# Hybrid SSD and chunk-MLP layer: x issued first, small parameters moved behind the first stage's last chunk, the last tile's h shared between two engines

## The chip, the core and the metric

The kernel runs on one core of one Trainium2 chip. A core has five engines, each with a queue of its own: PE (TensorE, the matrix products; its weight loads are listed apart as PEld), DVE (VectorE), ACT (ScalarE), POOL (GpSimd) and SP (SyncE, which here only issues transfers). Transfers between the chip's memory and the core's SBUF are issued on the queues of SP, ACT and POOL and are carried by 16 DMA engines that all of them share. The metric is the time of the program on the device in microseconds; less is better.

## The reference, cut to what matters

One layer (DEPTH is 1) over 256 latent tokens and 256 context tokens, width 2048. Context and latent tokens are normalized, modulated by adaLN with their own shift and scale, and projected; the latent ones then pass a two-sided SSD group and a chunked gating MLP group, and both meet in one output projection.

```
sc, scc = silu(c), silu(c_ctx)
shift, scale, gate = split(sc @ w_ada + b_ada, 3)          # the same for scc: shift_c, scale_c
hc = rmsnorm(ctx, g_pre) * (1 + scale_c) + shift_c
hx = rmsnorm(x, g_pre) * (1 + scale) + shift
zc = hc @ w_in[:, :XBC_W + DT_W]
zx = hx @ w_in                                              # XBC | dt | z_ssd | u | v | z_mlp
dt = softplus(z[dt columns] + dt_bias);  A = -exp(a_log)
xbc = silu(dwconv_rows(z[XBC columns], conv_w, conv_b))
y = ssd in both directions over xbc, dt, A  (latent starts from the context's final state)
y_a = rmsnorm((y + d_skip * xh) * silu(z_ssd), g_ssd)
y_b = rmsnorm(u * (w_s @ rmsnorm(v, g_v) + b_s) * silu(z_mlp), g_mlp)
out = x + gate * rmsnorm(concat(y_a, y_b) @ w_out, g_post)
```

## The kernel before

Every product with a large weight is made in three passes: each factor is split into a high part (a rounded copy, hi) and a low part (the rest, lo), and hi·hi, hi·lo and lo·hi are summed (mm3, lines 141 to 145).

The first stage, on which the change works, does four things at once. It reads x and ctx, transposed, into the tile xT (512 tokens, 16 tiles of 128 channels, four loads of 1 MB). It makes the norm's statistics. It computes shift and scale from w_ada. And it makes the first part of the projection for seven of the 32 column tiles of XBC and for the dt columns, tile of channels by tile of channels: row kt needs xT's tile kt, its shift and scale (hab), and the chunk wst[kt] of w_in (960 columns, 480 KB).

Transfers in that stage. On SP: sc2 (c and c_ctx, 16 KB, line 184), then xT (line 296), then, in the order of their need, chunks of w_ada ("ada", 1 MB each or two halves of 512 KB, lines 81 and 303) and of wst (lines 292 and 308). On ACT: pc (line 107), one tile with all parameters that lie along channels: 304 columns, of which the first 80 are b_ada and g_pre, used in the first stage, and the rest (from C_GSSD on) g_ssd, g_mlp, b_s, conv_w and conv_b, used later. In row 6 of the first stage ACT issues three more: dtc (dt_bias), A (a_log) and dsk (d_skip), lines 503 to 505, each a short vector spread over 128 partitions.

From line 286 on, PE, DVE, ACT and POOL keep the order in which the program writes their instructions (manual_schedule); ahead of that line, and on SP and the issuing of transfers, the builder orders them. The head of the stage (lines 314 to 361) reads so:

- ACT: silu of sc2 into sc (314), a square root of a constant (315), the copy of cb[0] (331), the first square, the copy of cb[1] (342), then the other squares of xT's even tiles (340).
- DVE: two diagonal tiles made from sc (328), then the squares of xT's odd tiles (338).
- PE: three filler products (warm, 322, 324), the two products of the diagonal tiles that spread c over all partitions (330), then per tile of xT the sum of its squares into pss (344), with a filler after each fourth (322, 346).
- Then pss is transposed (350), summed (352), its root and reciprocal taken (355, 356), and spread again (357, 358) into rb; ada_mm(0) and ada_mm(1) and two fillers follow on PE (359 to 361), and row 0 starts (line 452) when scale_x (388) and make_hs (400, 401) have made its h.

The rows (lines 414 to 445, a list of steps for each row) hold the products of row kt and, between them, the preparation of row kt + 1 or kt + 2: split_hi on ACT and split_lo and split_dt on DVE for the weights, make_h (four pieces on ACT, line 394) or make_hs (each of its two tensors half on ACT, half on DVE, lines 400 and 401) for h, make_hl (404) for its low part, ada_mm on PE and ada_part on DVE (265; its product goes to a junk tile cbj, which is yseg(0), a piece of the later output tile y) and ada_fin for shift and scale. From row 4 on two rows share one unit of shift and scale, so that each odd row prepares the next two tiles. In row 13 the weights of tile 15 come first (the whole chunk in one cast) and then its h in four pieces on ACT; in row 14 the low part of the weights (385) comes ahead of the low part of h (404). Row 15 ends the stage: psdt is copied and transposed to tokens, dtc is added (412), and the second stage, from line 507 on, starts with dt_all (A is used in line 650) and streams w_in's other columns, w_out and the gate's weights in 1 MB loads (line 81), in buffers that overlay those of the first stage.

Of the kernel before, what the change touches and what calls it, by code (L numbers as in the profile page):

```python
# [8 lines left out]
F32 = mybir.dt.float32  # L9
# [6 lines left out]
P = 128  # L16
D = 2048
KT = D // P
# [18 lines left out]
C_BADA, C_GPRE, C_GSSD, C_GMLP, C_BS, C_CW, C_CB, NPC = 0, 48, 64, 80, 96, 112, 272, 304  # L37
# [10 lines left out]
def tile_hybrid_ssd_mlp(  # L48
# [19 lines left out]
    nc = tc.nc  # L68
    ORDER = _tile_order()

    def mkpool(**kw):
        return tc.tile_pool(reuse_waits="tile", **kw)
# [29 lines left out]
    stp = st.enter_context(mkpool(name="stp", bufs=1, side="right"))  # L102
# [1 line left out]


    pc = cpool.tile([P, NPC], F32, name="pc")
    nc.scalar.dma_start(pc, pcols)
    dtc = stp.tile([P, 64], F32, name="dtc")

    ident = cpool.tile([P, P], F32, name="ident")  # L110
    make_identity(nc, ident)
    ones = cpool.tile([P, P], F32, name="ones")
# [34 lines left out]
    def bc(ap, axis, n):  # L147
        u = ap.unsqueeze(axis)
        shp = list(u.shape)
        shp[axis] = n  # L150
        return u.to_broadcast(shp)
# [4 lines left out]
    def yseg(j):  # L156
        return y[:, j // 4, (j % 4) * 512 : (j % 4 + 1) * 512]


    zq = (yseg(2), yseg(3), yseg(7)[:, 0:256])  # L160
    zdt = yseg(1)

    slot = (1, 2, 0, 3)
    zt, e = yseg(5)[:, 0:256], yseg(5)[:, 256:512]
# [1 line left out]
    s2 = yseg(4)[:, 0:256]  # L166
    at = y[:, 0, 256:512].rearrange("p (t h) -> p t h", t=4)
    fold = yseg(7)[:, 256:320]
    A = yseg(7)[:, 320:384]
    nc.vector.tensor_reduce(fold, ident.rearrange("p (g m) -> p m g", g=2), axis=mybir.AxisListType.X, op=ALU.add)  # L170
    acp = ctx.enter_context(mkpool(name="acp", bufs=2, space=PSUM))
    sps = ctx.enter_context(mkpool(name="sps", bufs=6, space=PSUM))
# [8 lines left out]
    sc = stp.tile([P, KT, 32], F32, name="sc")  # L181
    nc.vector.memset(sc, 0.0)
    sc2 = stp.tile([P, KT, 2], F32, name="sc2")
    nc.sync.dma_start(sc2, ccols)
    sqr = st3.tile([P, WST], F32, tag="wst", name="sqr")[:, 0:512], stp.tile([P, 512], F32, name="sqf")
    cb, cbj = (yseg(2), yseg(3)), yseg(0)
    part = {}
# [16 lines left out]
    def ada_load(*cs):  # L204
        for ci in cs:
            if ci >= 2 * NSING and ci % 4 == 3:
                ada_load2(ci)
            else:
                ada_raw[ci] = load_raw(wada[ci], f"ada_{ci}")
# [80 lines left out]
    def wst_load(kt):  # L290
        w = st3.tile([P, WST], F32, tag="wst", name=f"wst{kt}")
        nc.sync.dma_start(w, wst[kt])
        wraw[kt] = w
# [41 lines left out]
    for k in range(KT):  # L335
# [7 lines left out]
        g = k % 4  # L343
# [39 lines left out]
    def split_lo(kt, a=64, b=WST):  # L383
        hi, lo = sp0[kt]
        nc.vector.tensor_tensor(lo[:, a - 64 : b - 64], wraw[kt][:, a:b], hi[:, 64 + a : 64 + b].bitcast(F32), op=ALU.subtract)
# [28 lines left out]
    def row_steps(kt):  # L414


        m = [("m", i) for i in range(-1, NST)]
        if kt == KT - 1:
            out_ = [("m", i) for i in LAST]
            out_.insert(3, ("t", 0))  # L420
            for i in range(2):
                out_.insert(out_.index(("m", 4 + i)) + 1, ("z", i))
            return out_
        n = kt + 1
        c_, d_, l_, h_, e_ = [(w, n) for w in ("c", "d", "l", "h", "e")]
        m0 = [("m", -1), ("p", 0), ("p", 1), ("p", 2), ("w", 0), ("q", 0), ("q", 1), ("q", 2)]
        m1 = [("m", i) for i in range(3, NST)]
        u = (n - NSING) // 2 + NSING
        x = [("x", k) for k in XROW[kt]] if kt < len(XROW) else []
        p = 4 * u - 2 * NSING  # L430
        s_ = [("s", (n, i)) for i in range(2)]
        c1, c2, l1, l2 = [(w, n) for w in ("c1", "c2", "l1", "l2")]
        if n < NSING:
            r = [("r", 2 * n), ("r", 2 * n + 1)]
            q, f = (8, m1[1:2]) if n == 1 else (6, [])
            v = [("v", (NSING, i)) for i in range(4)] if n == NSING - 1 else []
            return (m0[:q] + f + r + [c1, ("k", n), d_, l1] + m1[:1] + [("g", n), ("o", n)] + s_ + [c2] + v[:1] + [e_, l2] + v[1:] + x
                    + m0[q:] + m1[1 + len(f):])
        if kt % 2 == 0:
            v = [("v", (u + 1, i)) for i in range(4)] if n + 1 < KT else []  # L440
            return [d_, l_] + v[:1] + [e_] + v[1:] + m0 + m1
        v = [("v", (u, i)) for i in range(4, 8)] + [("b", u)]
        a = [("a", c) for c in range(p + 1, p + 4)]
        t = v + [c1, ("f", u), d_, s_[0], l1, s_[1], e_, c2, l2, ("c", n + 1)] + x + [("h", (n + 1, i)) for i in range(2)]
        return m0 + m1[:1] + a + t + m1[1:]

    STEPS = {"a": ada_mm, "f": ada_fin, "v": lambda ui: ada_part(*ui), "b": ada_bias, "r": ada_rows, "x": scale_x, "e": make_hl, "s": lambda ni: make_hs(*ni), "k": ada_keep, "g": ada_sum, "o": ada_one,
# [7 lines left out]
    def step(kt, what, i):  # L455
        if what in STEPS:
            STEPS[what](i)
        elif what == "z":
            nc.vector.tensor_copy(zq[i], psx[4 + i])
        elif what == "t":  # L460
            dt_tok()
        elif i < 0:
            dt_mm(kt, 0)
            if kt == KT - 1:
                dt_mm(kt, 1)
        elif what == "w":
            dt_mm(kt, 1)
        elif what in "pq":
            whi, wlo = sp0[kt]
            wh = whi[:, (i + 1) * P : (i + 2) * P]  # L470
            if what == "p":
                nc.tensor.matmul(psx[i], lhsT=wh, rhs=hhi[kt], start=kt == 0, stop=False)
                nc.tensor.matmul(psx[i], lhsT=wlo[:, i * P : (i + 1) * P], rhs=hhi[kt], start=False, stop=False)
            else:
                nc.tensor.matmul(psx[i], lhsT=wh, rhs=hlo[kt], start=False, stop=False)
        else:
            whi, wlo = sp0[kt]
            mm3(psx[i], whi[:, (i + 1) * P : (i + 2) * P], wlo[:, i * P : (i + 1) * P], kt,
                kt == 0 and i < 6, kt == KT - 1 and i != 3, ORDER[FIRST[i]] >= 24)
# [13 lines left out]
    for kt in range(KT):  # L493
        cs = (2 * kt + 6, 2 * kt + 7) if kt + 3 < KT else ()
        q = 0 if kt < NSING - 2 or kt % 2 else 2
        ada_load(*cs[:q])
        if kt < KT - 2:
            wst_load(kt + 2)
        ada_load(*cs[q:])
        for what, i in row_steps(kt):  # L500
            step(kt, what, i)
        if kt == 6:
            nc.scalar.dma_start(dtc, dtp[0:1].partition_broadcast(P))
            nc.scalar.dma_start(A, dtp[1:2].partition_broadcast(P))
            nc.scalar.dma_start(dsk, dskip.partition_broadcast(P))

    st.close()
# [141 lines left out]
    def dt_all():  # L649
        nc.scalar.activation(A, A, AF.Exp)  # L650
        nc.vector.scalar_tensor_tensor(e, zt, -1.0, zt, op0=ALU.mult, op1=ALU.min)
        split_hi(0)
        nc.scalar.activation(e, e, AF.Exp)
        split_lo(0)
        split_hi(1)
        nc.vector.tensor_scalar(s1, e, 2.0, None, op0=ALU.add)
        nc.vector.reciprocal(s1, s1)
        split_hi(2)
        nc.vector.tensor_tensor(s1, s1, e, op=ALU.mult)
        nc.vector.tensor_tensor(s2, s1, s1, op=ALU.mult)  # L660
        nc.vector.tensor_scalar(pl, s2, 2.0 / 15.0, None, op0=ALU.mult)
        split_lo(1)
        for m in (13, 11, 9, 7, 5, 3):
            nc.vector.scalar_tensor_tensor(pl, pl, 2.0 / m, s2, op0=ALU.add, op1=ALU.mult)
        nc.vector.scalar_tensor_tensor(pl, pl, 2.0, s1, op0=ALU.add, op1=ALU.mult)
        nc.vector.scalar_tensor_tensor(dtt.rearrange("p t h -> p (t h)"), zt, 0.0, pl, op0=ALU.max, op1=ALU.add)
        nc.vector.scalar_tensor_tensor(at, dtt, -1.0, bc(A, 1, 4), op0=ALU.mult, op1=ALU.mult)
        split_lo(2)
# [462 lines left out]
    for blk in range(16):  # L1131
# [11 lines left out]
        for u in range(8):  # L1143
            whi, wlo = half(base + blk * 8 + u)
            for kk in range(2):
                k = 2 * u + kk
                w = slice(kk * 512, (kk + 1) * 512)
                for tk in range(2):
                    t = slice(256 + tk * P, 256 + (tk + 1) * P)
# [223 lines left out]
```

## Time and profile before

| what | us |
|---|---|
| median of 3 runs | 984.83 |
| lowest and highest of them | 984.71 and 985.9 |
| the profiled execution | 986.03 |
| its span, first to last instruction | 984.3 |
| PE, DVE, ACT, POOL busy in it | 974.9, 658.2, 498.3, 112.6 |
| memory read over the span | 204.20 MB, 210 GB/s |

A line of the profile's order of time gives the start and the duration of an instruction in us, its engine (ACTq and SPq are the issuing of ACT and SP), the line of the kernel, the operation, the tile written and the tiles read, the shape, how many instructions are merged into the line, and in brackets how long the engine stood idle before it and what ended that. A line of the waits gives who waited for whom, the sum in us, how often, and the longest. A line of the stretches gives the stretch and its length, then busy time and count for PE, PEld, DVE, ACT and POOL, the granted TensorE clock, the busy share of the DMA engines and GB/s. A line of the transfers gives the tile and its source, the queue, how many, the size of each and the median us from issue to landing.

### The profile page before, as it was taken

The numbers are of one execution on the slowest core, as the hardware profiler recorded it, in microseconds if no ns is written. First come the engines' busy times: TensorE is split into PE (matmuls) and PEld (weight loads), VectorE is DVE, ScalarE is ACT, GpSimd is POOL, SyncE is SP. The second block draws the span as 40 slices with busy tenths as digits, with TensorE's granted clock in tenths as the row PEclk, the third lists the DMA queues.
The fourth block names the chain that finished last, engine by engine and source line by source line (L and its number), as shares of the span: only waits on it lengthen the run. The fifth ranks groups of instructions, "written<-read, shape, count | busy, mean of one in ns | idle before, by whom it ended". The sixth has DMA issues, their size and how long they took to land.

```text
span 984.3 us, 13659 instructions
## 1 busy us (share of the span) xinstructions
PE 974.9 (99%) x5306; PEld 786.8 (80%) x5306; DVE 658.2 (67%) x1055; ACT 498.3 (51%) x759; POOL 112.6 (11%) x162
## 2 busy tenths in 40 slices
PE   9999999999999999999999999999999999999997
PEld 4688888787887878787888888887888888888885
DVE  6888798778876675656666766677555564445636
ACT  4344458666575454644445334555565553345522
POOL 0000002541462222133000000000000000000000
PEclk9999999999999999999999999999999999999999
DMA  9999943332333323146877767864455545556722
GB/s 371 416 414 414 403 165 133 114 131 86 129 112 136 138 86 129 61 154 241 305 298 280 269 243 288 298 258 171 173 195 187 176 169 211 189 195 236 276 87 86
DMA packets 32849, 207.26 MB, mean 211 GB/s; under 512 B 4224, under 2 KB 4480, under 8 KB 10128
## 3 DMA queue, kind: packets, MB, share of 16 engines
q1 hardware_dynamic: 29664, 192.71, 52.4%
q0 software_dynamic: 2112, 12.65, 3.6%
q10 hardware_dynamic: 1008, 1.02, 0.3%
q8 instruction: 42, 0.69, 0.3%
q14 instruction: 23, 0.19, 0.1%
HBM read 204.20 MB, written 2.16 MB: 210 GB/s over the span
## 4 chain that ended last, share of the span: by engine, by line
PE 72%; DMA 10%; issue 9%; DVE 5%; ACT 2%; POOL 1%; SPq 0%; DVEq 0%; ACTq 0%; POOLq 0%
PE psx L143 8%; PE psx L145 8%; PE psx L144 8%; PE pa L1150 8%; PE pa L1151 8%; PE pa L1152 8%; DMA wst<-in_wst_dram 5%; PE pm L1197 3%; PE pm L1199 3%; PE pm L1198 3%; PE pq L1199 2%; PE pq L1197 2%; PE pq L1198 2%; PE psc L820 1%; DMA gvb<-in_gv_dram 1%
## 5 line engine op out<-in xcount | busy, mean ns | idle before, releaser
L88 DVE TENSOR_TENSOR lo_w<-w,hi_w 128x1024 fp32r<-128x1024 f32 x173 | 210.3, 1223 | 139.9 <-ACT hi_w L87 139.9
L87 ACT CAST hi_w<-w 128x1024 fp32r<-128x1024 f32 x173 | 182.1, 1052 | 202.6 <-PE pa L1152 131.8
L1150 PE MATMUL pa<-hi_w,hhi 128*128 128x512 f32 x512 | 202.3, 395 | 0.0
L1151 PE MATMUL pa<-lo_w,hhi 128*128 128x512 f32 x512 | 199.4, 390 | 0.5 <-DVE lo_w L88 0.5
L1152 PE MATMUL pa<-hi_w,hlo 128*128 128x512 f32 x512 | 199.5, 390 | 0.0
L143 PE MATMUL psx<-hhi,hi_w 128*128 128x512 f32 (+1 forms) x400 | 153.4, 383 | 0.0
L145 PE MATMUL psx<-hhi,lo_w 128*128 128x512 f32 (+1 forms) x400 | 145.9, 365 | 0.0
L144 PE MATMUL psx<-hlo,hi_w 128*128 128x512 f32 (+1 forms) x400 | 145.7, 364 | 0.0
L1150 PEld LDWEIGHTS pa<-hi_w,hhi 128*128 128x128 f32 x512 | 96.1, 188 | 20.6 <-issue 1.6
L1151 PEld LDWEIGHTS pa<-lo_w,hhi 128*128 128x128 f32 x512 | 96.2, 188 | 20.2 <-DVE lo_w L88 0.9
L1152 PEld LDWEIGHTS pa<-hi_w,hlo 128*128 128x128 f32 x512 | 96.1, 188 | 20.3
L618 DVE SCALAR_TENSOR_TENSOR xbc<-psx,pc,xbc 128x248 f32<-128x248 f32 (+1 forms) x204 | 83.6, 471 | 34.9 <-ACT xbc L602 33.9
L543 DVE TENSOR_TENSOR lo_w<-w,hi_w 128x1024 fp32r<-128x1024 f32 x61 | 77.1, 1270 | 23.6 <-ACT hi_w L537 23.6
L143 PEld LDWEIGHTS psx<-hhi,hi_w 128*128 128x128 f32 x400 | 75.5, 189 | 13.4 <-issue 2.9
L145 PEld LDWEIGHTS psx<-hhi,lo_w 128*128 128x128 f32 x400 | 75.4, 189 | 12.5
L144 PEld LDWEIGHTS psx<-hlo,hi_w 128*128 128x128 f32 x400 | 75.7, 189 | 12.2 <-issue 1.7
L537 ACT CAST hi_w<-w 128x1024 fp32r<-128x1024 f32 x61 | 63.5, 1044 | 25.7 <-PE pa L1152 12.9
L1008 DVE SCALAR_TENSOR_TENSOR junk<-gate,cb 128x2048 bf16<-128x2048 f32 x16 | 36.6, 2290 | 29.2 <-DMA gate<-in_wada_dram 29.2
L1197 PE MATMUL pm<-hi_w,hhi 128*128 128x512 f32 x128 | 49.9, 390 | 0.0
L1198 PE MATMUL pm<-lo_w,hhi 128*128 128x512 f32 x128 | 49.9, 390 | 0.0
L1199 PE MATMUL pm<-hi_w,hlo 128*128 128x512 f32 x128 | 49.7, 389 | 0.0
L377 ACT CAST hi_st<-wst 128x448 fp32r<-128x448 f32 (+2 forms) x26 | 17.2, 679 | 56.9 <-DMA wst<-in_wst_dram 56.9
(269 smaller groups left out, 1392.2 us busy)
## 6 DMA issues: line engine op xcount, KB each, us to landing
w<-in_wlat_dram SPq DMA_DIRECT2D x64, 1024.0 KB, 4.8
w<-in_wout_dram SPq DMA_DIRECT2D x32, 1024.0 KB, 4.8
w<-in_wxbc_dram SPq DMA_DIRECT2D x25, 1024.0 KB, 4.8
ada<-in_wada_dram SPq DMA_DIRECT2D x24, 1024.0 KB, 13.3
gate<-in_wada_dram SPq DMA_DIRECT2D x16, 1024.0 KB, 5.8
ada<-in_wada_dram SPq DMA_DIRECT2D x16, 512.0 KB, 12.0
R<-acs POOLq DMA_DIRECT2D x8, 1024.0 KB, 5.0
wst<-in_wst_dram SPq DMA_DIRECT2D x15, 480.0 KB, 12.1
```

Source lines behind the costliest of these rows:

```text
L87: nc.scalar.copy(hi, raw)
L88: nc.vector.tensor_tensor(lo, raw, hi.bitcast(F32), op=ALU.subtract)
L143: nc.tensor.matmul(ps, lhsT=whi, rhs=hhi[k][:, s], start=start, stop=False)
L144: nc.tensor.matmul(ps, lhsT=whi, rhs=hlo[k][:, s], start=False, stop=False)
L145: nc.tensor.matmul(ps, lhsT=wlo, rhs=hhi[k][:, s], start=False, stop=stop)
L618: nc.vector.scalar_tensor_tensor(ao, zi, cw[:, k : k + 1], ao, op0=ALU.mult, op1=ALU.add)
L1150: nc.tensor.matmul(pa[tk], lhsT=hhi[k][:, t], rhs=whi[:, w], start=k == 0, stop=False)
L1151: nc.tensor.matmul(pa[tk], lhsT=hhi[k][:, t], rhs=wlo[:, w], start=False, stop=False)
L1152: nc.tensor.matmul(pa[tk], lhsT=hlo[k][:, t], rhs=whi[:, w], start=False, stop=k == KT - 1)
L1197: nc.tensor.matmul(p, lhsT=yh[:, t], rhs=whi[:, w], start=j == 0, stop=False)
L1198: nc.tensor.matmul(p, lhsT=yh[:, t], rhs=wlo[:, w], start=False, stop=False)
L1199: nc.tensor.matmul(p, lhsT=yl[:, t], rhs=whi[:, w], start=False, stop=hf == 0 and j == 15)
```

## The change

- x ahead: sc2 leaves SP's queue for ACT's, so that xT's loads are the first on SP. On ACT, sc2 stands behind pc.
- pc in two parts: the first 80 columns at the start, the other 224 in row 14 on ACT.
- dtc and A lose their places (a tile of its own, and a piece of yseg(7)) for two pieces of yseg(0), and are loaded after row 13's steps on SP, behind the last wst chunk, instead of in row 6 on ACT. dsk is loaded in row 14 on ACT, behind the rest of pc.
- In row 13, tile 15's h is made by make_hs (half on DVE) and ahead of the cast of its weights; in row 14, its low part is made first.

```
     pc = cpool.tile([P, NPC], F32, name="pc")
-    nc.scalar.dma_start(pc, pcols)
-    dtc = stp.tile([P, 64], F32, name="dtc")
-
+    nc.scalar.dma_start(pc[:, 0:C_GSSD], pcols[:, 0:C_GSSD])
...
+    dtc, A = yseg(0)[:, 0:64], yseg(0)[:, 64:128]
...
-    A = yseg(7)[:, 320:384]
...
-    nc.sync.dma_start(sc2, ccols)
+    nc.scalar.dma_start(sc2, ccols)
...
         if kt % 2 == 0:
             v = [("v", (u + 1, i)) for i in range(4)] if n + 1 < KT else []
-            return [d_, l_] + v[:1] + [e_] + v[1:] + m0 + m1
+            return ([d_, l_] + v[:1] + [e_] + v[1:] if v else [e_, d_, l_]) + m0 + m1
...
-        t = v + [c1, ("f", u), d_, s_[0], l1, s_[1], e_, c2, l2, ("c", n + 1)] + x + [("h", (n + 1, i)) for i in range(2)]
+        g = [("c", n + 1)] + x + [("h", (n + 1, i)) for i in range(2)]
+        if n == KT - 2:
+            g = [("s", (n + 1, i)) for i in range(2)] + g[:1]
+        t = v + [c1, ("f", u), d_, s_[0], l1, s_[1], e_, c2, l2] + g
...
-        if kt == 6:
-            nc.scalar.dma_start(dtc, dtp[0:1].partition_broadcast(P))
-            nc.scalar.dma_start(A, dtp[1:2].partition_broadcast(P))
+        if kt == KT - 3:
+            nc.sync.dma_start(dtc, dtp[0:1].partition_broadcast(P))
+            nc.sync.dma_start(A, dtp[1:2].partition_broadcast(P))
+        if kt == KT - 2:
+            nc.scalar.dma_start(pc[:, C_GSSD:], pcols[:, C_GSSD:])
             nc.scalar.dma_start(dsk, dskip.partition_broadcast(P))
```

## The prediction

> **What bounds the kernel now.** I read the page first, then the stretches, then the order of time at both ends of the first stage.
>
> ```profile
> span 984.3 us, 13659 instructions
> PE 974.9 (99%) x5306; PEld 786.8 (80%) x5306; DVE 658.2 (67%) x1055; ACT 498.3 (51%) x759; POOL 112.6 (11%) x162
> ...
> q10 hardware_dynamic: 1008, 1.02, 0.3%
> ```
>
> TensorE is busy for 99% of the span, so a gain or loss at the start reaches the end unless a later wait swallows it. The span is 984.3 us, this execution 986.03 (1.7 lie around the span), the median 984.83. I make the sum as a difference and set it on the median.
>
> The view by stretches, cut where the norm statistics end (16.84), where the first product starts (21.85) and where the first stage ends (126.10):
>
> ```profile
> 8.00:16.80 8.80, 8.45 (x41) 2.03 (x40) 4.06 (x6) 5.37 (x10) 0.00 (x0) 1.00 1.00 415
> ...
> 21.85:126.10 104.25, 103.47 (x1061) 82.95 (x1061) 88.19 (x215) 44.41 (x81) 0.00 (x0) 1.00 1.00 405
> 126.10:984.30 858.20, 851.03 (x4064) 696.08 (x4062) 557.88 (x814) 443.95 (x662) 110.23 (x147) 1.00 0.51 183
> ```
>
> From 21.85 to 126.10 the DMA share is 1.00 and PE is busy 103.47 of 104.25 us: transfers and products are both full, tied to within little. So how much PE waits for transfers in there decides what a shift of either is worth. The waits of the weight loads, 15 to 130 us:
>
> ```profile
> PEld psdt L452 <- ACT hhi L400: 1.4, 4, 0.8
> ...
> PEld psada L256 <- DMA ada<-in_wada_dram: 1.0, 2, 0.5
> PEld psada L227 <- DMA ada<-in_wada_dram: 1.0, 2, 0.6
> ...
> PEld psdt L452 <- DVE hlo L404: 0.4, 1, 0.4
> ```
>
> The 0.8 of the first row is row 0's own start; without it they are 3.0 us. A weight load runs ahead of its product, so less is lost: at the last one 0.4 of idle load became about 0.25 of idle PE (the two psdt products quoted below start 0.48 apart; the mean of the long stretch above is 851.03 / 4064 = 0.21). At that ratio some 1.8 us of this stage are waits that would go if transfers led by more. Bounds: 0.5 and 3.0.
>
> **The head, which the change rearranges.** The order of time before the first product:
>
> ```profile
> 0.81 0.38 SPq L184 DMA_DIRECT2D sc<-in_ccols_dram  x1
> ...
> 1.25 2.24 SPq L296 DMA_DIRECT2D xT<-in_xch_dram  x4
> ...
> 2.80 1.28 ACT L314 ACT_TABLE_LOAD   x1 [2.80 <-DMA sc<-in_ccols_dram]
> ...
> 4.36 0.69 DVE L328 TENSOR_TENSOR y<-ident,sc 128x512 f32<-128x512 f32 x1 [0.51 <-ACT sc L314]
> ...
> 6.40 2.33 PE L330 MATMUL pscb<-y,ones 128*128 128x512 f32 x4
> 6.41 0.34 PEld L330 LDWEIGHTS pscb<-y,ones 128*128 128x128 f32 x1 [0.52 <-issue]
> ...
> 7.26 0.21 PEld L330 LDWEIGHTS pscb<-y,ones 128*128 128x128 f32 x1 [0.52 <-DVE y L338]
> 7.71 0.19 PEld L330 LDWEIGHTS pscb<-y,ones 128*128 128x128 f32 x1 [0.24 <-issue]
> 7.91 0.59 ACT L331 COPY y<-pscb 128x512 f32<-128x512 f32 x1 [2.07 <-PE pscb L330]
> ...
> 8.92 0.58 ACT L342 COPY y<-pscb 128x512 f32<-128x512 f32 x1
> ...
> 9.39 1.16 ACT L340 ACTIVATE y<-xT 128x512 f32<-128x512 f32 x2
> ...
> 11.07 0.70 PE L322 MATMUL psw<-ones 128*128 128x256 f32 x2
> ...
> 15.56 0.62 PE L344 MATMUL pss<-y,ones 128*32 128x512 f32 x1
> ...
> 16.56 1.13 PE L322 MATMUL psw<-ones 128*128 128x512 f32 x2
> 16.84 0.72 DVE L350 STREAM_TRANSPOSE y<-pss 128x512 f32<-128x512 f32 x1 [1.68 <-PE pss L344]
> ```
>
> All of ACT, VectorE and TensorE stand in hand-written order behind sc: ACT's table load waits for it, the two diagonal tiles of L328 stand ahead of VectorE's squares, the L330 products ahead of the squares' sums, both copies ahead of ACT's squares. Today sc lands so early that the diagonal tile, ready at 5.05, waits until 6.40 behind the filler products of L322.
>
> **Part 1: x first, sc2 behind pc on ACT's queue.** x is issued at 0.81 instead of 1.25: the transfer stream comes 0.44 us sooner. ACT gets one issue more, while it waits anyway. pc shrinks from 304 to 80 columns, 152 to 40 KB: 0.28 us of stream at 415 GB/s. That is the gain. The cost: the two small loads now travel while x fills all 16 engines. What that does is shown by the three small loads that ACT issues in row 6, under a full stream:
>
> ```profile
> ada<-in_wada_dram SPq DMA_DIRECT2D x16, 512.0 KB, 12.0
> ...
> dtc<-in_dtp_dram ACTq DMA_DIRECT2D x1, 32.0 KB, 5.7
> y<-in_dtp_dram ACTq DMA_DIRECT2D x1, 32.0 KB, 6.8
> sc<-in_ccols_dram SPq DMA_DIRECT2D x1, 16.0 KB, 1.9
> dsk<-in_dskip_dram ACTq DMA_DIRECT2D x1, 16.0 KB, 7.6
> ```
>
> (size, and us from issue to landing), and the issues in order of time:
>
> ```profile
> 68.27 0.34 ACTq L503 DMA_DIRECT2D dtc<-in_dtp_dram  x1
> ...
> 68.65 0.45 ACTq L504 DMA_DIRECT2D y<-in_dtp_dram  x1
> 69.13 0.45 ACTq L505 DMA_DIRECT2D dsk<-in_dskip_dram  x1
> ```
>
> They land at 73.97, 75.45 and 76.73: 1.48 and 1.28 us apart, for 32 and 16 KB, so it isn't bytes. ACT's queue made 1008 packets for seven transfers (these three, pc, three stores): 144 each, nine for each of 16 engines. The big stream then had 4 KB rows; at 415 GB/s over 16 engines one takes 0.158 us, and nine take 1.42. So a small load gets one packet in for each packet of the stream. x has 8 KB rows, 0.316 us each: nine turns are 2.84 us, and pc and sc2, one behind the other, need 5.7. The Trainium skill, "DMA: Bandwidth & Descriptors", section on queues, rings and completion order, has the engines alternate between queues a whole packet of some 9 to 17 descriptors at a time; by that a small load would pass in one turn. The trace disagrees: 1.48 and 1.28 us instead of about 0.16.
>
> So ACT wakes at 2.80 + 5.7 = 8.5 less about 0.3 for turns in which x only signals: 8.2. Bounds: 6.5 if half of pc gets in before x flows; 10.3 if the 2.3 us of dtc's landing that neither its turns (1.48) nor an empty-queue landing (1.9, sc) explains come on top.
>
> At 8.2 (5.4 later) the diagonal tile starts at 9.76 and is ready at 10.5; the L330 products start there, 4.1 later than 6.40, and the copy comes at 12.0. What clock do they get? The fillers end at 6.40 as now, then TensorE idles 4 us. The L330 loads are 0.85 apart before 7.26 and 0.45 after, so the full rate came only then. With the passes as now the second copy comes at 13.0, the third square (9.39 now) at 13.5, out at 14.1. With all four passes at 0.85 the second copy waits until 14.15, that square is out at 15.2. The Trainium skill, "TensorE: Matmul & The Clock Gate", Part 1, says that an idle window brings the half rate back, which would speak for the slower; no row of before shows such a gap.
>
> From that square on TensorE paces, since ACT and VectorE have their squares ready by then or soon after: four groups of four sums, 1.00 each (15.56 to 16.56), two short fillers between them at 0.70 (the row of 11.07) and a long one at 1.13 (the like of 16.56): 6.5, and 0.28 to the transpose. It starts at 20.9 or 22.0, or 23.0 if the first group is slow too, against 16.84: 4.1 to 6.2 later. I take 5.0. What follows until 21.85 is a chain of small steps whose other inputs come no later, so row 0 starts 5.0 later. From there the transfers lead by 5 more, and the 1.8 us of waits go. Net **+3.2 us** at the stage's end; bounds 4.1 − 1.7 (the 6.5 wake) − 3.0 = −0.6, and 6.2 + 2.1 (the 10.3 wake) − 0.5 = +7.8, each only if all its parts meet; by pairs that I find likely, +1.5 to +5.
>
> **Part 2: parameters behind the last chunk.** Row 6 loses three issues on ACT and three small loads (27 turns of little data); while PE paces that is worth nothing. The new places, and the end of the stage:
>
> ```profile
> 112.85 23.75 SPq L81 DMA_DIRECT2D w<-in_wxbc_dram  x6
> 116.94 1.00 ACT L377 CAST hi_st<-wst 128x960 fp32r<-128x960 f32 x1 [0.52 <-DMA wst<-in_wst_dram]
> 119.95 0.69 DVE L404 TENSOR_TENSOR hlo<-xT,hhi 128x512 fp32r<-128x512 f32 x1 [0.75 <-ACT xT L394]
> 120.22 0.39 PE L452 MATMUL psdt<-hhi,hi_st 128*128 128x512 f32 x1
> 120.70 0.50 PE L452 MATMUL psdt<-hlo,hi_st 128*128 128x512 f32 x1
> 123.30 1.04 ACT L537 CAST hi_w<-w 128x1024 fp32r<-128x1024 f32 x1
> 127.81 0.78 ACT L602 ACTIVATE xbc<-psx,pc 128x512 f32<-128x512 f32 x1
> ```
>
> dtc and A now go into the junk tile of VectorE's ada sums, so on SP they wait for the last of these sums, which stands in row 13 beside the ada products that the first w load waits for today; the w loads queue behind both issues, 0.8 us (0.34 and 0.45 in row 6). The first w is cast only at 123.30, 10 us after its issue of 112.85; that covers it, and also a product group of about 1 us more to wait for, should the 256 bytes that dtc's tile frees shift the buffers that w overlays. dtc and A are needed only when psdt's last product (120.70) has been copied. The rest of pc and dsk follow the cast of 116.94 on ACT, which then has nothing until that copy: two issues, 0.9 us, are hidden; landing within 7.6 of 118 makes 125.6, before the first tap at 127.81. Cost nothing; without that cover it is at most 1 to 2 us in a stretch where convolution steps queue on VectorE.
>
> **Part 3: last tile's h shared, ahead of its weights.** Today the last cast (1.00) and then ACT's four pieces stand ahead of the hlo of 119.95. The change does h first, half on VectorE (which idled 0.75 there), and hlo ahead of the weight's low part. The 0.25 us wait of the second psdt product goes. It is among the 1.8, not counted twice. The low part ends later on VectorE by about one hlo (0.7), still before its first use three products on.
>
> **Rivals.** *sc lands early* (the engines let a small load through at once): then the head starts 0.44 sooner, sc2's later issue is hidden by the 1.35 us between 5.05 and 6.40, and transfers lead by 0.28 for pc plus 0.2 for row 6's 80 KB, so waits of that size go too: 0.44 + 0.28 + 0.2 + 0.25 = 1.2 us faster, **983.6**. It decides if sc arrives before about 4.3. For it: at 0.81 both queues are empty and pc may get its nine packets in before x flows. Against: the spacing in row 6. It is also what the rule of the Trainium skill on queues, named above, would make of this change. *sc2 goes ahead of pc, or pc slips in before x*: nine turns, wake at 2.80 + 2.84 = 5.6, diagonal ready at 7.9, products 1.5 later than 6.40, or 2.5 with slow passes; less the 1.8 of waits that is −0.3 to +0.7: about **985.0**, no difference. For it: the order of the two issues is the builder's, since these queues aren't in the hand-written order; against: SP's two kinds of load stand in the order of the code. *The parameters block the w loads*: would need more than the 10 us of cover; left at 2 in 100.
>
> **How the numbers follow.** Forecast 65 in 100: 984.83 + 3.2 = **988.0**, own range 986.3 to 989.8. Early sc 17, no difference 16, blocking 2. The range 984.3 to 990.4 leaves out the early case and the far tail. A measurement of this kernel tells about 0.2%, 2.0 us, from no change. The forecast lies above 986.8 in 58 of its 65, the early case below 982.9 in 4 of 17, the blocked case above: faster 0.04, same 0.36, slower 0.60.
>
> **What would show it.** Right: ACT's first table load waiting for sc until 7 to 10 us; PE idle from 6.4 to past 9; squares' last sum past 20; row 0 near 27; no waits on ada afterwards; no hlo wait at the last row; span longer by 2 to 4. Wrong: sc landing near 3 and row 0 before 21.85; or row 0 late and the stage's end not, which would mean more of the stage was waiting than I read; or ACT or the w casts waiting for pc, dtc or w after 120.

## The result and the profile after

| kernel | median, us | lowest to highest | runs |
|---|---|---|---|
| before | 984.88 | 984.71 to 985.9 | 6 |
| after | 988.31 | 988.06 to 991.39 | 6 |

The ratio is 1.0038, with a 95% interval of 1.0025 to 1.0051: the change makes the kernel 3.4 us (0.4%) slower. The forecast was 988.0, in the range of 984.3 to 990.4. The profiled execution of after took 988.24, of which 1.7 lie around its span. The profiled execution of before (986.03) lay 1.2 above its median, and in it one weight load waited 0.9 us for VectorE at about 572 us, far behind the change; in the execution of after none waited there. So the two spans differ by only 2.2, and I compare the first stage instead.

The page of after and its stretches, cut where the granted clock changes, where the norm statistics end and at the first stage's first and last product (us, then busy time and count for PE, PEld, DVE, ACT and POOL, the clock, the share of the DMA engines, GB/s):

```profile
span 986.5 us, 13662 instructions
...
PE 973.9 (99%) x5306; PEld 788.0 (80%) x5306; DVE 658.2 (67%) x1057; ACT 497.2 (50%) x757; POOL 112.5 (11%) x162
```

```profile
5.90:9.30 3.40, 0.42 (x1) 0.00 (x0) 0.72 (x4) 0.62 (x1) 0.00 (x0) 1.00 1.02 423
9.30:16.10 6.80, 5.12 (x10) 1.50 (x12) 3.35 (x6) 4.79 (x9) 0.00 (x0) 0.50 1.01 422
16.10:22.80 6.70, 6.70 (x37) 1.85 (x35) 3.33 (x6) 3.04 (x6) 0.00 (x0) 1.00 1.02 406
27.80:129.20 101.40, 101.23 (x1061) 83.41 (x1062) 88.49 (x217) 43.74 (x79) 0.00 (x0) 1.00 0.96 387
```

PE's busy time is 1.0 less than before's 974.9 in a span that is 2.2 longer. That is a sum of opposites. Up to row 0, TensorE was idle for 5.8 us instead of 1.5 and busy for 1.6 longer; in the rows its busy time fell by 2.2 (103.47 to 101.23). The stretch up to row 0, in before and in after:

```profile
0.00:21.85 21.85, 20.38 (x185) 7.82 (x185) 12.16 (x28) 9.91 (x18) 2.39 (x15) 1.00 0.91 367
...
0.00:27.80 27.80, 22.01 (x185) 8.02 (x185) 12.02 (x28) 9.81 (x18) 2.37 (x15) 0.88 0.94 380
```

Two things are new in the stretches. TensorE ran at half clock from 9.30 to 16.10, just when the products that spread c came. And the rows of the stage took 101.40 us instead of 104.25, with a DMA share of 0.96 instead of 1.00: the transfers have slack now, and TensorE no longer waits for them.

The order of time in the head of after:

```profile
0.81 2.10 SPq L294 DMA_DIRECT2D xT<-in_xch_dram  x4
0.81 0.41 ACTq L107 DMA_DIRECT2D pc<-in_pcols_dram  x1
...
1.25 0.45 ACTq L182 DMA_DIRECT2D sc<-in_ccols_dram  x1
...
6.10 0.18 DVE L130 TENSOR_SCALAR bab<-pc 128x16 f32<-128x16 f32 x1 [4.48 <-DMA pc<-in_pcols_dram]
...
8.68 1.28 ACT L312 ACT_TABLE_LOAD   x1 [8.68 <-DMA sc<-in_ccols_dram]
...
10.24 0.69 DVE L326 TENSOR_TENSOR y<-ident,sc 128x512 f32<-128x512 f32 x1 [3.42 <-ACT sc L312]
...
10.98 3.78 PE L328 MATMUL pscb<-y,ones 128*128 128x512 f32 x4 [4.67 <-DVE y L326]
...
13.10 0.58 ACT L329 COPY y<-pscb 128x512 f32<-128x512 f32 x1 [1.38 <-PE pscb L328]
...
14.80 0.58 ACT L340 COPY y<-pscb 128x512 f32<-128x512 f32 x1 [0.59 <-PE pscb L328]
...
22.79 0.72 DVE L348 STREAM_TRANSPOSE y<-pss 128x512 f32<-128x512 f32 x1 [1.74 <-PE pss L342]
...
27.79 0.50 PE L453 MATMUL psdt<-hhi,hi_st 128*128 128x512 f32 x1
```

ACT wakes at 8.68 instead of 2.80, because c now arrives after pc, and pc after 6 us. The four product passes take 3.78 us instead of 2.33. The transpose starts 5.95 later (22.79 against 16.84) and row 0 starts 5.94 later (27.79 against 21.85). The other end of the stage:

```profile
116.06 0.33 SPq L504 DMA_DIRECT2D y<-in_dtp_dram  x1
...
117.30 2.07 SPq L81 DMA_DIRECT2D w<-in_wxbc_dram  x4
...
120.24 0.34 ACTq L507 DMA_DIRECT2D pc<-in_pcols_dram  x1
...
120.61 0.50 ACTq L508 DMA_DIRECT2D dsk<-in_dskip_dram  x1
...
126.39 1.04 ACT L540 CAST hi_w<-w 128x1024 fp32r<-128x1024 f32 x1
...
129.19 0.40 PE L141 MATMUL psx<-hhi,hi_w 128*128 128x512 f32 x1
...
130.88 0.78 ACT L605 ACTIVATE xbc<-psx,pc 128x512 f32<-128x512 f32 x1
```

The first product of the second stage starts at 129.19, 3.1 after before's 126.1. The first cast of w (126.39 against 123.30) and the first tap of the convolution (130.88 against 127.81) are 3.1 later too: nothing waits for the parameters in their new places. So of 5.94 us lost in the head, 2.9 are given back in the rows, and 3.1 arrive (in one trace of each kernel; the medians differ by 3.4). In the waits of the weight loads from 15 to 130 us, the rows that named ada and hlo in before are gone, and the psdt row holds little beyond row 0's own 0.8:

```profile
PEld psada L225 <- issue: 1.1, 3, 0.4
PEld psdt L453 <- ACT hhi L398: 1.0, 2, 0.8
```

### The profile page after: what moved, and what is told of

Its sections match the earlier page's. It is cut to its first block, busy times and chain, and to the rows that moved or that the text cites. A ratio compares the mean times of both kernels' runs of the same rounds, so it can differ in the third digit from the quotient of the medians.

```text
span 986.5 us, 13662 instructions
## 1 busy us (share of the span) xinstructions
PE 973.9 (99%) x5306; PEld 788.0 (80%) x5306; DVE 658.2 (67%) x1057; ACT 497.2 (50%) x757; POOL 112.5 (11%) x162
## 4 chain that ended last, share of the span: by engine, by line
PE 96%; ACT 2%; DVE 1%; DMA 1%; issue 0%; ACTq 0%
PE pa L1153 12%; PE pa L1155 12%; PE pa L1154 12%; PE psx L141 9%; PE psx L143 9%; PE psx L142 9%; PE pm L1200 3%; PE pm L1201 3%; PE pm L1202 3%; PE pq L1200 2%; PE pq L1201 2%; PE pq L1202 2%; PE psada L254 2%; PE psc L823 1%; PE pso L876 1%; PE psx L476 1%
## 5 line engine op out<-in xcount | busy, mean ns | idle before, releaser
L775 ACT ACTIVATE R<-R,y 128x128 f32<-128x128 f32 x128 | 38.8, 391 | 0.0
```

## The experiments

My theory: c and pc travel behind x's 8 KB rows (each row is a packet, as the profile counts them), one turn for each of their own; ACT wakes late by that; everything in the head stands behind ACT's wake; the rows then swallow what they used to wait for transfers. Rivals: x's early start or the parameters' new places cost something by themselves; the order of the two small loads decides (rival 2 of the prediction); the half clock, not the late c, is the larger part.

In this table "wake" is the start of ACT's first table load, "row 0" and "end" are the first product of row 0 and the first of the second stage, from each kernel's trace.

| kernel | median, us | ratio to before (95%) | wake | row 0 | end | row 0 to end |
|---|---|---|---|---|---|---|
| before | 984.88 | | 2.80 | 21.85 | 126.12 | 104.27 |
| after | 988.31 | 1.0038 (1.0025 to 1.0051) | 8.68 | 27.79 | 129.19 | 101.40 |
| sc_first | 984.42 | 0.9994 (0.9986 to 1.0003) | 2.72 | 21.54 | 125.37 | 103.83 |
| sc_ahead_of_pc | 987.10 | 1.0023 (1.0014 to 1.0032) | 5.87 | 26.42 | 127.85 | 101.43 |
| x_half_rows | 986.62 | 1.0020 (1.0011 to 1.0029) | 6.65 | 26.17 | 127.60 | 101.43 |
| more_fillers | 986.61 | 1.0017 (1.0008 to 1.0026) | 8.86 | 26.26 | 127.67 | 101.41 |
| only_x_first | 989.12 | 1.0039 (1.0025 to 1.0052) | 9.65 | 28.69 | 130.10 | 101.41 |
| third_small_load | 991.26 | 1.0060 (1.0048 to 1.0073) | 11.68 | 30.73 | 132.17 | 101.44 |
| sc_ahead_bab_late | 985.60 | 1.0005 (0.9996 to 1.0013) | 6.42 | 24.69 | 126.09 | 101.40 |
| squares_first | 984.31 | 0.9990 (0.9982 to 0.9999) | 1.73 | 23.29 | 125.14 | 101.85 |
| only_last_tile | 984.85 | 0.9995 (0.9986 to 1.0003) | 2.88 | 21.38 | 125.73 | 104.35 |
| no_fillers_in_sums | 988.06 | 1.0026 (1.0017 to 1.0035) | 9.26 | 26.34 | 127.76 | 101.42 |

(squares_first loads its first table for the squares, so its wake has nothing to do with c. The runs of before beside the four rows from only_x_first to squares_first had a median of 985.16, beside the last two 985.58; ratios are each to its own, and since before's own medians differ by 0.7 us, medians of different groups are comparable only to about that.)

**sc_first: the order of the first loads undone, all else kept.**

```
-    nc.scalar.dma_start(sc2, ccols)
+    nc.sync.dma_start(sc2, ccols)
```

> The changed kernel with one line back: sc2 is issued on SP ahead of x, as before; pc stays cut and all else stays changed. Theory (the late sc2 is the whole loss): ACT's first table load starts near 2.8 us again instead of 8.7, row 0 near 21.8 instead of 27.8, and the time is that of the kernel before less the wait of the last tile and the smaller pc: 984.4 (984.0 to 984.9). Rival (the loss lies in the later parts: parameters behind the last chunk, last tile's h): the time stays near 988.3.

Measured: 984.42, c there at 2.72, row 0 at 21.54. The whole loss is gone, so it comes from the exchange of x and c; pc in two parts, the late parameters and part 3 together cost nothing that can be told, and gain nothing either. This edit also puts x back behind c. That x's early start isn't what costs is shown by squares_first below, which has x first and is not slower.

```profile
2.72 1.28 ACT L312 ACT_TABLE_LOAD   x1 [2.72 <-DMA sc<-in_ccols_dram]
```

**sc_ahead_of_pc: the two loads on ACT's queue exchanged.**

```
+    sc2 = stp.tile([P, KT, 2], F32, name="sc2")
+    nc.scalar.dma_start(sc2, ccols)
     pc = cpool.tile([P, NPC], F32, name="pc")
     nc.scalar.dma_start(pc[:, 0:C_GSSD], pcols[:, 0:C_GSSD])
```

> The changed kernel with sc2 issued ahead of pc on ACT's queue. Theory (one packet of a small load for each packet of x): sc2 has nine turns to wait instead of eighteen, ACT wakes at 5.5 to 6.0, row 0 comes at 23 to 24.5, and the stage's waits swallow most of it: 985.2 (984.4 to 986.2). Rival (ACT's queue as a whole starts late, or its loads wait for whole loads of x): the wake stays near 8.7 and the time near 988.3.

Measured: 987.10, against the theory's time. The wake came at 5.87, as the turns say, and yet row 0 at 26.42. The order of time shows why:

```profile
5.87 1.28 ACT L312 ACT_TABLE_LOAD   x1 [5.87 <-DMA sc<-in_ccols_dram]
...
8.45 0.18 DVE L132 TENSOR_SCALAR bab<-pc 128x16 f32<-128x16 f32 x1 [6.83 <-DMA pc<-in_pcols_dram]
...
9.08 0.68 DVE L326 TENSOR_TENSOR y<-ident,sc 128x512 f32<-128x512 f32 x1
...
9.82 3.63 PE L328 MATMUL pscb<-y,ones 128*128 128x512 f32 x4 [3.28 <-DVE y L326]
```

Two tiny VectorE instructions that make bab from pc stand ahead of the diagonal tile in VectorE's order. With c first they wait for pc until 8.45, and the diagonal tile behind them starts at 9.08 instead of about 7.4. The order of the two loads only exchanges which engine waits. I had not seen this in the trace of before, where pc lands early as well.

**sc_ahead_bab_late: the same, and those two instructions moved behind the squares.**

```
-    nc.vector.tensor_scalar(bab[:, :, 0], pc[:, C_BADA + 16 : C_BADA + 32], 1.0, None, op0=ALU.add)
-    nc.vector.tensor_copy(bab[:, :, 1], pc[:, C_BADA : C_BADA + 16])
...
+    nc.vector.tensor_scalar(bab[:, :, 0], pc[:, C_BADA + 16 : C_BADA + 32], 1.0, None, op0=ALU.add)
+    nc.vector.tensor_copy(bab[:, :, 1], pc[:, C_BADA : C_BADA + 16])
     rb, ss4 = yseg(4), yseg(5)
```

> The kernel with sc2 ahead of pc on ACT's queue, and VectorE's two bias instructions, which wait for pc, moved from ahead of the diagonal tiles to behind the squares. Theory (in the kernel with sc2 ahead, sc came at 5.87 but VectorE stood behind pc until 8.45): the diagonal tile starts at 7.4 instead of 9.0, row 0 comes at 23 to 25, and the stage's waits swallow nearly all that is left: 984.9 (984.2 to 985.8). Rival (the half clock and the lateness of sc alone made that kernel's 987.1): no change.

Measured: 985.60, the end of the stage at 126.09. Against sc_ahead_of_pc row 0 and the end come 1.7 sooner although c came 0.55 later. Of this, 1.1 is the diagonal tile that no longer waits for pc (7.97 instead of 9.08); the rest is that the passes behind it took 2.83 instead of 3.63, since fewer of them fell into the half clock. The kernel is level with before: rival 2 of the prediction gave 985.0 and would have been right if only c had mattered.

```profile
7.97 0.69 DVE L324 TENSOR_TENSOR y<-ident,sc 128x512 f32<-128x512 f32 x1 [5.89 <-ACT sc L310]
...
8.72 2.83 PE L326 MATMUL pscb<-y,ones 128*128 128x512 f32 x4 [2.19 <-DVE y L324]
...
17.86 0.17 DVE L345 TENSOR_SCALAR bab<-pc 128x16 f32<-128x16 f32 x1
```

**third_small_load: after, with 16 KB more between pc and c on ACT's queue** (a piece of the parameters that after loads in row 14).

```
     nc.scalar.dma_start(pc[:, 0:C_GSSD], pcols[:, 0:C_GSSD])
+    nc.scalar.dma_start(pc[:, C_GSSD:C_BS], pcols[:, C_GSSD:C_BS])
...
-            nc.scalar.dma_start(pc[:, C_GSSD:], pcols[:, C_GSSD:])
+            nc.scalar.dma_start(pc[:, C_BS:], pcols[:, C_BS:])
```

> The changed kernel with one more small load on ACT between pc's first part and sc2: 32 of pc's later columns (16 KB), which row 14's load then leaves out. Theory (nine turns of 8 KB packets for each small load): ACT wakes 2.6 to 2.9 us later, at 11.3 to 11.7, and since the stage has no wait left that could swallow it, the time rises by as much: 991.0 (990.4 to 991.5). Rival (bytes decide): 16 KB are 0.04 us, no change, 988.3.

Measured: the wake at 11.68, 3.0 after that of after, and 991.26. The prediction's nine turns of 0.316 make 2.84. Within this trace, c came 5.14 after pc (6.54) with the new load between them, 2.57 for each of the two loads, as in after (6.10 to 8.68); the rest of the 3.0 is that pc came 0.44 later. By bytes alone 16 KB would be 0.04 us at 415 GB/s, so this is a price for packets.

```profile
11.68 1.28 ACT L313 ACT_TABLE_LOAD   x1 [11.68 <-DMA sc<-in_ccols_dram]
```

**x_half_rows: after, with x in eight loads of 512 KB,** so that its rows are 4 KB.

```
-    for t in range(4):
-        nc.sync.dma_start(xT[:, 4 * t : 4 * t + 4, :].rearrange("p k t -> p (k t)"), xch[t])
+    for t in range(8):
+        nc.sync.dma_start(xT[:, 2 * t : 2 * t + 2, :].rearrange("p k t -> p (k t)"),
+                          xch[t // 2][:, (t % 2) * 1024 : (t % 2 + 1) * 1024])
```

> The changed kernel with x in eight loads of 512 KB instead of four of 1 MB: rows of 4 KB instead of 8 KB, the same bytes. Theory (turns by packet): eighteen turns cost 2.8 us instead of 5.7, ACT wakes at 5.6 to 6.2, row 0 at 23 to 24.5, time 985.3 (984.5 to 986.3). Rival (bytes or whole loads of x decide, or a late start of ACT's queue): the wake stays near 8.7 and the time near 988.3.

Measured: the wake at 6.65, 2.0 earlier; 986.62. The step from pc's arrival to c's is 1.4 (5.27 to 6.65) instead of 2.6, half, as the turns have it, and equal to the 1.48 and 1.28 of the prediction's row 6. Its first part did not halve (pc's rows start between 2.47 and 4.72 in the trace, between 2.79 and 5.49 in after; why isn't shown), so the wake is 0.5 later than expected, and the four passes again take the 3.78 us of the half clock: against after the time gained 1.7 and not 3.

```profile
5.27 0.18 DVE L130 TENSOR_SCALAR bab<-pc 128x16 f32<-128x16 f32 x1 [3.66 <-DMA pc<-in_pcols_dram]
...
6.65 1.28 ACT L313 ACT_TABLE_LOAD   x1 [6.65 <-DMA sc<-in_ccols_dram]
...
8.95 3.78 PE L329 MATMUL pscb<-y,ones 128*128 128x512 f32 x4 [3.23 <-DVE y L327]
```

**more_fillers: after, with eight filler products in place of three,** so that TensorE is busy while it waits for c.

```
-    warm(512, 512, 512)
+    warm(*[512] * 8)
```

> The changed kernel with eight filler products of 512 columns instead of three at the very start, so that TensorE is not idle while it waits for sc. sc still lands late. Theory (of the loss, a part is the half clock that the idle time brings back): the two products behind sc take half as long, the second copy comes at about 13.1 instead of 14.8, row 0 near 26.2, and the time falls to 986.6 (986.2 to 987.3). Rival (the lateness of sc alone): no change, 988.3.

Measured: 986.61, with c as late as in after (8.86). The first two of the stretches above show the clock at 1.00 here:

```profile
5.90:9.30 3.40, 3.40 (x9) 1.52 (x8) 0.72 (x4) 0.44 (x1) 0.00 (x0) 1.00 1.03 428
9.30:16.10 6.80, 5.73 (x17) 1.45 (x15) 4.56 (x8) 6.33 (x12) 0.00 (x0) 1.00 1.00 420
```

and the passes take 1.98 instead of 3.78:

```profile
11.16 1.98 PE L328 MATMUL pscb<-y,ones 128*128 128x512 f32 x4 [0.73 <-DVE y L326]
...
21.25 0.72 DVE L348 STREAM_TRANSPOSE y<-pss 128x512 f32<-128x512 f32 x1 [1.75 <-PE pss L342]
```

The transpose comes 1.54 sooner although c came 0.18 later, so the half clock is worth 1.7 us of after's 5.94 in the head; the late c alone makes the other 4.2. The third rival is refuted as the larger part, and confirmed as half of the net loss: the rows still swallow 2.9, so this kernel loses 1.7 where after loses 3.4.

**only_x_first: before, with c moved to ACT behind the whole of pc,** and nothing else.

```
-    nc.sync.dma_start(sc2, ccols)
+    nc.scalar.dma_start(sc2, ccols)
```

> The kernel before with one line changed: sc2 goes to ACT's queue behind the whole pc, so that x is first on SP. All later parts of the change are absent. Theory (the late sc2 is the whole loss): ACT wakes near 8.7, row 0 near 27.8, and the time is the changed kernel's plus the last tile's 0.25 us: 988.5 (988.0 to 989.0). Rival (the later parts cost something of their own): less than 987.5.

Measured: 989.12. One moved line makes the whole loss. pc is read at 7.10 instead of 6.10 and the wake is at 9.65 instead of 8.68: cutting pc to its first 80 columns, which the prediction valued at 0.28 of stream, seems to have saved up to 1.0 in this place. With one trace each that isn't shown: the same head gave wakes from 8.68 to 9.26 in three kernels.

```profile
9.65 1.28 ACT L314 ACT_TABLE_LOAD   x1 [9.65 <-DMA sc<-in_ccols_dram]
```

**only_last_tile: before, with part 3 alone** (the diff's lines in row_steps).

> The kernel before with part 3 alone (the last tile's h shared and ahead of its weights, its low part first). Theory: the head stays as it is (row 0 at 21.85, 0.1 either way); the wait of the second psdt product for hlo, 0.25 of idle PE, goes, the other waits for transfers stay; the stage ends at 125.9 and the median is 984.6 (984.3 to 984.9), which this measurement can't tell from 0. Rival: the last rows are also bound by wst's transfer, so that the wait only changes its name: 984.9, the stage's end at 126.1.

Measured: 984.85, not to be told from before. The hlo row is gone from the waits, and the ada rows grew from 2.0 to 2.7 in all:

```profile
PEld psada L227 <- DMA ada<-in_wada_dram: 1.4, 2, 0.7
...
PEld psada L256 <- DMA ada<-in_wada_dram: 1.3, 4, 0.6
PEld psdt L455 <- ACT hhi L400: 1.2, 3, 0.8
```

Row 0 happened to start 0.47 sooner and the end 0.39 sooner, so row 0 to end is no shorter (104.35 against 104.27). That is the rival's picture, a stage bound by its transfers in which one wait takes the place of another; but 0.1 us is beneath what one trace of each can show.

**squares_first: after, with c's work behind x's squares,** so that nothing in the head waits for c: silu and the square root come after ACT's square of tile 6, the diagonal tiles and their products after the sum of tile 11, both copies after ACT's last square.

```
-    nc.scalar.activation(sc[:, :, 0:2], sc2, AF.Silu)
-    nc.scalar.activation(sc2[:, 0, 0:1], epsc, AF.Sqrt)
...
+            if k == 6:
+                nc.scalar.activation(sc[:, :, 0:2], sc2, AF.Silu)
+                nc.scalar.activation(sc2[:, 0, 0:1], epsc, AF.Sqrt)
...
+        if k == 11:
+            spread_c()
+        elif g == 3:
```

> The changed kernel with sc's work moved behind the squares: silu and the diagonal tiles come after the squares of the first chunks, the two products that spread c take the place of the long filler, and both copies follow ACT's last square; x stays first, sc2 stays late. Theory (late sc costs only because everything in the head stands behind it): row 0 at 20.8 to 21.8 although sc still lands near 8, and the time is below both kernels: 983.9 (983.3 to 984.6). Rival (small loads among x's packets slow x itself, or the head is slow for another reason): 986 or more.

Measured: 984.31, ratio 0.9990 (0.9982 to 0.9999): the only one whose interval lies below 1, by 0.1%; it just excludes no change, so that one such among ten may be chance. c, which still lands late, is no longer waited for (the row of its table load at 9.98 names no wait):

```profile
6.25 1.15 ACT L336 ACTIVATE y<-xT 128x512 f32<-128x512 f32 x2 [3.24 <-DMA xT<-in_xch_dram]
...
9.98 1.28 ACT L338 ACT_TABLE_LOAD   x1
...
13.59 1.05 PE L341 MATMUL pss<-y,ones 128*32 128x512 f32 x4 [1.61 <-ACT y L336]
...
18.29 0.72 DVE L351 STREAM_TRANSPOSE y<-pss 128x512 f32<-128x512 f32 x1 [2.92 <-PE pss L341]
...
23.29 0.50 PE L456 MATMUL psdt<-hhi,hi_st 128*128 128x512 f32 x1
```

Row 0 was expected near 21 and came at 23.29, since ACT's two table loads now stand between its squares (TensorE waits 1.61 for the next one) and the products of c ahead of the last sums. It cost nothing: the end of the stage is at 125.14, and sc_first with row 0 at 21.54 ends no sooner, at 125.37. In both the DMA share of the rows is 1.00, so I take this end for the bound that the transfers set. Every kernel with row 0 from 24.69 on has 101.40 to 101.44 from row 0 to the end and ends at 126.09 or later. So as an estimate the end of this stage is the later of some 125.2 and row 0 + 101.4, and a head that is done by about 23.8 is soon enough. Before (126.12) and only_last_tile (125.73) lie up to 0.9 above that first bound, and no kernel has row 0 between 23.29 and 24.69.

**no_fillers_in_sums: after, without the fillers between the groups of squares' sums.**

```
-        if g == 3:
-            warm(512 if k > 8 else 256)
```

> The kernel after without the fillers between the groups of squares' sums (two short ones of 0.70 and one long of 1.13, or twice that at half clock). Theory: in the late head TensorE paces from the second copy on, so that without them the transpose comes 2.5 earlier than 22.79 until ACT's squares pace (seven at 0.58 behind the copy of 14.80, the last out at about 19), so at 20.3, row 0 at 25.3, the stage's end at 126.7 and the median at 985.8 (985.3 to 986.5). Rival: without the fillers the clock stays at half past 16.1, and into the first row, which takes as much as they cost: 988 or more, row 0 to the stage's end longer than 101.4.

Inconclusive for the time. From the second copy to the transpose it took 5.96 (15.38 to 21.34) instead of 7.99, so the fillers do pace the head, by 2.0 rather than 2.5; and the clock was back at 1.00 from 17 on, against the rival:

```profile
15.38 0.58 ACT L340 COPY y<-pscb 128x512 f32<-128x512 f32 x1 [0.59 <-PE pscb L328]
...
21.34 0.72 DVE L346 STREAM_TRANSPOSE y<-pss 128x512 f32<-128x512 f32 x1 [1.21 <-PE pss L342]
```

The stage ended 1.4 sooner than in after, and yet the median is 988.06 (986.37 to 989.48). In the profiled execution TensorE lost 1.3 again shortly before 648, in a wait for VectorE that after doesn't have there:

```profile
PE ptm L1058 <- DVE vt L1118: 1.3, 1, 1.3
```

Whether that wait is in the other executions, and whether the earlier end brings it, stays open.

## Why the prediction was right

**Right, with the mechanism.** c waits for pc's and its own turns between x's rows, ACT wakes late, the whole head shifts, and the rows of the stage give a part back.

One step of the argument was wrong. The Trainium skill, "DMA: Bandwidth & Descriptors", section on queues, rings and completion order, has an engine drain a whole packet of some 9 to 17 descriptors before it turns to another queue. The prediction let the small load pass as a whole by that rule but the stream by a single row, and so came to 0.16 us. If the stream's turn is nine rows too, the estimate by that rule of the Trainium skill is nine rows of x for each small load, 2.84 us, the same price as row by row. So the spacing in row 6, third_small_load (+3.0 us for 16 KB) and x_half_rows (2.6 to 1.4) show that a small load pays for rows of the stream, but don't tell the two ways of taking turns apart. The trace's record of single packets does (no view above lists it): in after c's 128 rows start between 5.40 and 8.03 us in 16 series of eight, one for each DMA engine, with 0.31 to 0.33 us from row to row. One row of x takes 0.31 there. So the turns go row by row, as the prediction took it, and the trace differs from the rule of the Trainium skill.

**The wake:** 8.2 expected, 8.68 measured, within 6.5 to 10.3. The diagonal tile (9.76 expected, 10.24) and the products (10.5, 10.98) are late by the same 0.48. The same head gave 8.86 in more_fillers and 9.26 in no_fillers_in_sums, so a single execution tells it to about half a us. Two sizes in it were off, in opposite directions. A small load took 2.6 (6.10 to 8.68) rather than 2.84, eight rows and not nine: the ninth packet is a signal of 4 bytes that goes out right behind the eighth row. And pc's first row started at 2.79 in after, where it started at 1.90 in before; only the prediction's upper bound, with the unexplained 2.3 of dtc's landing, has room for that.

**The head was mis-sized:** 5.0 expected, 5.94 measured. Half of the difference is the wake. The other half is the clock, where the prediction took the middle between passes at the present rate (second copy at 13.0) and all at the slow one (14.15): the slow one is what happened (14.80, with 0.48 for the wake and 0.2 more). The gap of TensorE was judged right and then hedged. The rule of the Trainium skill, "TensorE: Matmul & The Clock Gate", Part 1, that was cited there was borne out in the main: the rate fell 3 us into the gap, and stayed down for 6.8 us, twice the 3.4 us of its window, before products had filled one. The window ahead of the fall wasn't idle throughout, though: TensorE was busy for 0.42 of its 3.40 us.

**The waits were mis-sized too:** 1.8 expected to go, 2.87 went (104.27 to 101.40), near the bound of 3.0. The step that failed is the scaling: 3.0 us of waiting weight loads were cut to 1.8 by the ratio of idle load to idle PE at one product. But PE's idle time in these rows fell only from 0.78 (104.25 less 103.47) to 0.17, while its *busy* time fell from 103.47 to 101.23 for the same 1061 products. The profile page's warning that the ends of products are modelled applies: I take it that most of the waiting stood in the busy column. The sum of the weight loads' waits (3.0) was the better measure here of what a lead of the transfers is worth.

The two errors (0.94 too little lost, 1.07 too little regained) cancel, and that is luck: it is why +3.2 meets a measured +3.07 at the stage's end so closely. With both sized right, the sum would have been 5.9 − 2.9 = 3.0.

**Part 2** cost nothing, as worked out: the w loads go out at 117.30, 4.5 later than before where the stage is 3.1 later, and the cast and the first tap move with the stage; sc_first, with all of part 2, is not slower than before. The last of the parameters, issued at 120.24 and 120.61, end nobody's wait. **Part 3** did remove the hlo wait, and by itself that is nothing that could be measured (only_last_tile).

**The rivals.** *sc lands early* did not happen (8.68, and it would have needed 4.3). Nor would the rule of the Trainium skill on queues have made it happen, as the prediction has it: with nine rows of x to a turn, c comes late by that rule too. Its price, 1.2 us, wasn't measured, since no kernel has both c and x early; sc_first, where c is early, x isn't, and all the rest of the change stands, gains 0.5 on the medians, with an interval that takes in no change at all. *sc2 ahead of pc* was given 985.0; with the loads in that order the time is 987.10. The wake was sized right there (5.6, measured 5.87), but VectorE's order was not followed past the load: bab waits for pc ahead of the diagonal tile. *The parameters block the w loads* did not happen.

## What to carry over

A small load that the head of a kernel stands behind goes out ahead of the big stream, also when that delays the stream: here 0.4 us of earlier x cost 5.9 us of later c, and only because the stage had 2.9 us of waits for transfers did 3.1 remain. When loads change their order, follow each one to its first reader in that engine's order, and to what stands behind that reader. And before an early start is bought, ask which of two bounds the stage ends on: moving the work that needs the late data behind work whose data is already there (squares_first, 984.31) took the loss away where the exchange of loads alone made it (988.31).

## What the hardware showed that was not expected

- A 16 KB load between a small one and c, under x's stream, put c 3.0 us later (third_small_load), about as much as 1.25 MB of stream take at 415 GB/s.
- A gap of TensorE of under 5 us (4.67 in after) brought 6.8 us at a clock of 0.50; the passes in it took 3.78 instead of 1.98, and with five more fillers the half clock was gone (988.31 to 986.61). In sc_ahead_bab_late a gap of 2.19 was enough for 3.4 us of half clock (9.73 to 13.14), though TensorE was busy for 1.23 of the 3.42 us ahead of it.
- The rest of pc and dsk, issued on ACT's queue at 120.24 and 120.61 under the stream of w (DMA share 0.97 from 120.20 to 130.50), took 7.7 and 9.8 us from issue to landing, while c takes 1.9 on empty queues in before. The two small loads that SP issued at 116.06, when the DMA engines had little to do (share 0.04 from 116.00 to 117.40), took 3.6:

```profile
pc<-in_pcols_dram ACTq DMA_DIRECT2D x1, 120.0 KB, 7.7
...
y<-in_dtp_dram SPq DMA_DIRECT2D x2, 32.0 KB, 3.6
...
dsk<-in_dskip_dram ACTq DMA_DIRECT2D x1, 16.0 KB, 9.8
```
